# A hybrid decoder trunk on one core: the masks of the attention scores added in PSUM by VectorE in fp32, in place of matmuls of identity and mask

## The chip, the cores and the metric

The kernel runs on one core of a Trainium2 chip. The metric is the device time of one execution in microseconds; the runs of the kernel before took 1051.38, 1052.3 and 1052.58 us, a median of 1052.3. All inputs and the output are fp32.

## The reference

Two layers over 256 tokens of width 1024. Each layer has four sub-layers, each between two RMS norms: a SwiGLU feed-forward of width 2816, a mixer, a second feed-forward, and a gated embedding. The mixer is the part that the change touches:

```python
# eight MLA heads, causal; scores in fp32
s = (einsum('bqhd,bkhd->bhqk', qn, k_nope) + einsum('bqhd,bkd->bhqk', qr, k_rope)) * scale
s = where(causal, s, NEG)            # NEG = -1e30
w = softmax(s); o = einsum('bhqk,bkhd->bqhd', w, v)
# eight heads of dilated windows: (window, dilation) of (128, 1), (512, 4), (2048, 16)
for window, dilation in DIL_CONFIGS:
    ...
    s = where(valid, s, NEG); lse = m + log(den)
o = sum over configs of softmax(lse) * o_config
merged = concat(rmsnorm(o_mla), rmsnorm(o_dil)); return merged @ w_out
```

With 256 tokens each token of a dilated head sees the keys that any of the three configurations admits, weighted by how many of them do; the kernel computes it as one softmax whose exponentials are multiplied by that count.

## The kernel before

The tokens lie in two tiles of 128 (t = 0 and 1). Activations and weights are split into hi + lo parts of 12 significant bits (fp32r), and a product is three matmuls: hi by hi, lo by hi, hi by lo (`mm3`, lines 320 to 323; `proj`; lines 479 and on for the feed-forward's second product). The class `Weights` loads a raw tile by SyncE's queue, and a "tick" splits one piece of it: ScalarE writes hi (line 152), VectorE writes lo (line 153). Each phase of matmuls is emitted by `run`, and a table PLAN, written by hand, says after which step of the phase a tick falls, and after which step other work (transposes, copies) is put in. The order on every engine is the order of emission; each engine works through its queue in that order. `split_t` transposes 128x128 blocks through PSUM ("tp"), ScalarE copies them to hi (xh, line 401) and VectorE takes the difference (xl, line 402).

PSUM has two pools of four banks of 512 fp32 columns: ps_mm (tag "mm") and ps_acc. A matmul into a bank waits until the last reader of the tile that had it is done.

In the mixer, `scores(kind, t)` is called four times in a layer: "m" 0, "m" 1, "d" 0 and "d" 1, called m0, m1, d0 and d1 below. For t = 0 a bank holds 4 heads of 128 keys, for t = 1 two heads of 256 keys: 2, 4, 2 and 4 banks. For each bank TensorE first opens it with a matmul of a bf16 identity and the bf16 mask (lines 654 and 658): for "m" and for t = 0 the causal mask on the last 128 keys of each head, for d1 the mask on all 256 keys. It then adds the heads' scores to that (line 666). In the dilated calls two banks are worked on together, since their heads lie on the two halves of the 128 partitions. VectorE takes the maximum (mx, line 669) and scales it (line 670), and ScalarE the exponentials (p, line 673).

`p_t` transposes the probabilities (line 683); its copies out of PSUM (pt) are on ScalarE or VectorE for "m" (line 204 or 202), and for "d" a product with the counts on VectorE (lines 688 and 692). `p_v` multiplies with the values (o, line 706); VectorE takes the reciprocal of the sums (rc, line 711) and divides (om, line 716), ScalarE sums the squares (junk, line 354), GpSimd makes the norm's factor (rs, line 348), and VectorE scales (on, line 720). `o_t` transposes that into xh and xl. Around d1 the emission is: `p_v("d", 0)`; `scores("d", 1)`; the first half of the output product of tile 1 (f) with a tick after its step 5, `o_t("d", 0)` at step 6 and `p_t("d", 1)` at step 7; `p_v("d", 1)`.

Other names in the rows: kmt and qmt are the transposed keys and queries of the MLA heads, kdt and qdt those of the dilated heads, dt their transposes in PSUM, km and qm what is transposed, vm and vd the values, dk and dv the projections of the dilated keys and values, qu and ku the MLA up-projections.

`setup_late` loads the mask and the tables once, in the first feed-forward, and casts identity and mask to bf16 (lines 296 and 297).

## Time and profile before

| | |
|---|---|
| median of the runs | 1052.3 us |
| span of the profiled execution | 1052.4 us |
| instructions | 13069 |
| TensorE clock granted | 0.999 |
| DMA, mean | 180 GB/s |
| VectorE busy | 645.8 us, 61% |
| ScalarE busy | 528.9 us, 50% |

The span runs from the first to the last instruction. An engine's busy time is the time in which one of its instructions runs; matmuls overlap in the pipeline, so their listed durations add up to more than the time they take, and the distance of their starts is the better measure. The mean of a group is in nanoseconds, all else in microseconds. A row of the timeline has the start, the duration, the engine, the line of the kernel, the instruction with out<-in, the shape, the count of merged instructions, and in brackets the idle time of the engine just before, with what ended it. "issue" there is time for which the profile shows no wait. PE is TensorE, PEld its weight loads, DVE VectorE, ACT ScalarE, POOL GpSimd.

### The profile page before, as it was taken

How to read it: one execution, taken by the hardware profiler on the slowest of the kernel's cores; microseconds unless marked ns; L12 is line 12 of the kernel's file. 1: busy time of each engine (PE TensorE's matmuls, PEld its weight loads, DVE VectorE, ACT ScalarE, POOL GpSimd, SP SyncE). 2: the span in 40 equal slices, each digit the busy share in tenths (PEclk: the TensorE clock that was granted, in tenths of full speed). 3: DMA queues.
4: the chain of work that ended last, by engine and by line, in shares of the span. 5: the costliest groups of instructions: out<-in, count | busy, mean ns of one | idle time of the engine just before them, and what ended most of it. 6: DMA issues, size and time to landing. Idle time of an engine off the chain costs nothing.

```text
span 1052.4 us, 13069 instructions
## 1 busy us (share of the span) xinstructions
PE 1037.1 (99%) x5168; PEld 867.0 (82%) x5168; DVE 645.8 (61%) x819; ACT 528.9 (50%) x744; POOL 51.1 (5%) x123
## 2 busy tenths in 40 slices
PE   8999999999999999999999999999999999999997
PEld 5889888878888898888878888888888888988886
DVE  4765554778677455456776545557877864555474
ACT  5544443555556444444665444445564654444463
POOL 0000000210020000000110000002000200000011
PEclk9999999999999999999999999999999999999999
DMA  8864546364227564554547645455532575545601
GB/s 321 304 227 168 193 164 211 106 222 160 82 94 272 191 213 160 201 200 160 200 160 259 212 169 200 153 163 168 180 120 82 190 275 184 198 162 172 227 21 40
DMA packets 86158, 189.02 MB, mean 180 GB/s; under 512 B 3665, under 2 KB 15313, under 8 KB 86098
## 3 DMA queue, kind: packets, MB, share of 16 engines
q1 hardware_dynamic: 86098, 188.20, 52.0%
q8 instruction: 40, 0.66, 0.2%
q14 instruction: 20, 0.16, 0.0%
HBM read 187.13 MB, written 1.05 MB: 179 GB/s over the span
## 4 chain that ended last, share of the span: by engine, by line
PE 92%; DVE 3%; ACT 2%; DMA 1%; issue 1%; POOL 0%; SPq 0%; DVEq 0%; POOLq 0%; ACTq 0%
PE acc L479 23%; PE u L323 8%; PE u L321 8%; PE u L322 8%; PE g L321 7%; PE g L323 7%; PE g L322 7%; PE tp L398 3%; PE o L706 2%; PE sc L666 1%; DVE lo L153 1%; PE gt L323 1%; PE gt L322 1%; PE gt L321 1%; PE f L321 1%; PE f L323 1%
## 5 line engine op out<-in xcount | busy, mean ns | idle before, releaser
L153 DVE TENSOR_TENSOR lo<-raw,hi 128x1024 fp32r<-128x1024 f32 (+1 forms) x338 | 405.1, 1214 | 204.2 <-ACT hi L152 194.1
L152 ACT ACTIVATE hi<-raw 128x1024 fp32r<-128x1024 f32 (+1 forms) x338 | 347.2, 1049 | 170.9 <-PE u L323 79.3
L479 PE MATMUL acc<-hi,hid 128*128 128x512 f32 x704 | 201.5, 392 | 0.0
L479 PEld LDWEIGHTS acc<-hi,hid 128*128 128x128 f32 x704 | 131.7, 188 | 27.4
L321 PE MATMUL u<-hi,xh 128*128 128x512 f32 (+1 forms) x384 | 145.3, 379 | 0.0
L323 PE MATMUL u<-hi,xl 128*128 128x512 f32 (+1 forms) x384 | 143.2, 373 | 0.0
L322 PE MATMUL u<-lo,xh 128*128 128x512 f32 (+1 forms) x384 | 143.0, 372 | 0.0
L321 PE MATMUL g<-hi,xh 128*128 128x512 f32 (+1 forms) x360 | 135.0, 375 | 2.3 <-ACT xh L401 2.3
L323 PE MATMUL g<-hi,xl 128*128 128x512 f32 (+1 forms) x360 | 134.6, 374 | 0.0
L322 PE MATMUL g<-lo,xh 128*128 128x512 f32 (+1 forms) x360 | 134.5, 374 | 0.0
L479 PE MATMUL acc<-lo,hid 128*128 128x512 f32 x352 | 118.3, 395 | 0.0
L323 PEld LDWEIGHTS u<-hi,xl 128*128 128x128 f32 x384 | 72.3, 188 | 13.0
L322 PEld LDWEIGHTS u<-lo,xh 128*128 128x128 f32 x384 | 72.4, 188 | 12.1
L321 PEld LDWEIGHTS u<-hi,xh 128*128 128x128 f32 x384 | 72.3, 188 | 12.0
L321 PEld LDWEIGHTS g<-hi,xh 128*128 128x128 f32 x360 | 68.5, 190 | 14.4 <-ACT xh L401 2.7
L322 PEld LDWEIGHTS g<-lo,xh 128*128 128x128 f32 x360 | 68.5, 190 | 12.3 <-DVE lo L153 0.5
L323 PEld LDWEIGHTS g<-hi,xl 128*128 128x128 f32 x360 | 68.4, 190 | 12.4 <-DVE xl L402 0.6
L479 PEld LDWEIGHTS acc<-lo,hid 128*128 128x128 f32 x352 | 66.2, 188 | 13.2
L401 ACT ACTIVATE hid<-tp 128x512 fp32r<-128x512 f32 (+1 forms) x48 | 27.0, 563 | 95.6 <-PE tp L398 95.6
L453 DVE SCALAR_TENSOR_TENSOR hm<-u,rs,silu 128x512 f32<-128x512 f32 (+1 forms) x48 | 33.7, 703 | 65.1 <-PE u L323 65.1
L448 ACT ACTIVATE silu<-g,rs 128x512 f32<-128x512 f32 (+1 forms) x48 | 31.3, 652 | 81.3 <-PE g L323 81.2
L402 DVE TENSOR_TENSOR hid<-tp,hid 128x512 fp32r<-128x512 f32 (+1 forms) x48 | 31.0, 647 | 44.0 <-ACT hid L401 43.6
(216 smaller groups left out, 1195.0 us busy)
## 6 DMA issues: line engine op xcount, KB each, us to landing
raw<-in_ffn_up SPq DMA_DIRECT2D x44, 1024.0 KB, 5.1
raw<-in_ffn_down SPq DMA_DIRECT2D x44, 1024.0 KB, 5.0
raw<-in_ffn_gate SPq DMA_DIRECT2D x43, 1024.0 KB, 5.2
raw<-in_w_in SPq DMA_DIRECT2D x12, 1024.0 KB, 5.2
raw<-in_w_out SPq DMA_DIRECT2D x8, 1024.0 KB, 5.1
raw<-in_w_ple_gate SPq DMA_DIRECT2D x8, 1024.0 KB, 5.1
gain<-in_norm_gains SPq DMA_DIRECT2D x15, 512.0 KB, 4.0
raw<-in_w_in SPq DMA_DIRECT2D x4, 832.0 KB, 5.2
```

The source lines that it names most:

```text
L152: self.nc.scalar.activation(hv, raw, AF.Copy)
L153: self.nc.vector.tensor_tensor(lv, raw, hv.bitcast(F32), op=ALU.subtract)
L321: nc.tensor.matmul(ps, sh, wh, start=first, stop=False)
L322: nc.tensor.matmul(ps, sh, wl, start=False, stop=False)
L323: nc.tensor.matmul(ps, sl, wh, start=False, stop=last)
L398: nc.tensor.transpose(ps[:, j * P : (j + 1) * P], src[:, (b0 + j) * P : (b0 + j + 1) * P], ident)
L401: nc.scalar.activation(hv, v, AF.Copy)
L402: nc.vector.tensor_tensor(dl[:, k0 + b0 : k0 + b0 + nb, :], v, hv.bitcast(F32), op=ALU.subtract)
L448: nc.scalar.activation(s[:, :w], ps[:, :w], AF.Silu, scale=rx[t][:, 0:1])
L453: nc.vector.scalar_tensor_tensor(hm[:, :w], ps[:, :w], rx[t][:, 0:1], sg[t][:, c0 : c0 + w], op0=ALU.mult, op1=ALU.mult)
L479: nc.tensor.matmul(accs[t][n], hid[t][x][:, b, :], ws[w][:, 0, n * 512 : (n + 1) * 512], start=first and x + w == 0, stop=final and x == 1)
L706: nc.tensor.matmul(dst, pt[:, b * P : (b + 1) * P], va[:, kb, hd, :], start=kb == 0, stop=kb == t)
```

## The change

The bank's first matmul is no longer that of identity and mask. Each head's score matmul opens its own columns, and before the maximum VectorE adds the mask, now kept in fp32, to the bank in place. The bf16 identity and the casts go; the mask is loaded straight into its fp32 tile. All else in the diff is comments, so line numbers behind it are up to six lower in the changed kernel.

```diff
-    identb = const.tile([P, P], BF16, name="identb")
-    mask = const.tile([P, 2, P], BF16, name="mask")
+    mask = const.tile([P, 2, P], F32, name="mask")
...
-        mask32 = k2("mask32")[:, : 2 * P]
-        nc.sync.dma_start(mask32, a["mask"].rearrange("p c q -> p (c q)"))
+        nc.sync.dma_start(mask.rearrange("p c q -> p (c q)"), a["mask"].rearrange("p c q -> p (c q)"))
...
-        nc.vector.tensor_copy(identb, ident)
-        nc.vector.tensor_copy(mask.rearrange("p c q -> p (c q)"), mask32)
...
-                for v in vs:
-                    if kind == "m" or t == 0:
-                        nc.tensor.matmul(v[:, :, nk - P :], identb, mask[:, 1, None, :].to_broadcast([P, n, P]),
-                                         start=True, stop=True)
-                    else:
-                        mk = mask.rearrange("p c q -> p (c q)")[:, None, :].to_broadcast([P, n, nk])
-                        nc.tensor.matmul(v, identb, mk, start=True, stop=True)
...
-                        nc.tensor.matmul(v[:, i, :], q, k, start=False, stop=True, skip_group_check=True)
+                        nc.tensor.matmul(v[:, i, :], q, k, start=True, stop=True)
                 for v in vs:
                     mx = stat.tile([P, 4], F32, tag="mx", name="mx")
+                    if kind == "m" or t == 0:
+                        d, mk = v[:, :, nk - P :], mask[:, 1, None, :].to_broadcast([P, n, P])
+                    else:
+                        d, mk = v, mask.rearrange("p c q -> p (c q)")[:, None, :].to_broadcast([P, n, nk])
+                    nc.vector.tensor_tensor(d, d, mk, op=ALU.add)
                     nc.vector.tensor_reduce(mx[:, :n], v, axis=AX.X, op=ALU.max)
```

The order of VectorE at the end of d1 in layer 0, in the kernel before (mx from the last two banks, then the split of a weight, the low part of `o_t("d", 0)`, and the products of `p_t("d", 1)`):

```order
L669 TENSOR_REDUCE mx<-sc 128x2
L670 TENSOR_SCALAR mx<-mx 128x2
L669 TENSOR_REDUCE mx<-sc 128x2
L670 TENSOR_SCALAR mx<-mx 128x2
L153 TENSOR_TENSOR lo<-raw_2131,hi 128x1024
L402 TENSOR_TENSOR xl_112<-tp,xh_110 128x512
L692 TENSOR_TENSOR pt<-pt,mult 128x512 x4
```

The same place in the change:

```order
L662 TENSOR_TENSOR sc<-sc,mask 128x512
L663 TENSOR_REDUCE mx<-sc 128x2
L664 TENSOR_SCALAR mx<-mx 128x2
L662 TENSOR_TENSOR sc<-sc,mask 128x512
L663 TENSOR_REDUCE mx<-sc 128x2
L664 TENSOR_SCALAR mx<-mx 128x2
L153 TENSOR_TENSOR lo<-raw_2127,hi 128x1024
L398 TENSOR_TENSOR xl_111<-tp,xh_109 128x512
L686 TENSOR_TENSOR pt<-pt,mult 128x512 x4
```

Each bank has one instruction more, ahead of its maximum, and the split, xl and pt stand behind all four of them.

The order of TensorE through the second half of d1 in layer 0, before:

```order
L658 MATMUL sc<-mask,identb 128x512
L666 MATMUL sc<-kdt,qdt 128x256 x4
L658 LDWEIGHTS identb
L658 MATMUL sc<-mask,identb 128x512
L658 LDWEIGHTS identb
L658 MATMUL sc<-mask,identb 128x512
L666 MATMUL sc<-kdt,qdt 128x256 x4
L321 MATMUL f_2498<-hi,xh_111 128x512
```

And in the change, with the last products of `p_v("d", 0)` ahead:

```order
L319 MATMUL f_2369<-hi,xl_111 128x512
L700 MATMUL o_2431<-vd,pt 128x65 x4
L700 MATMUL o_2432<-vd,pt 128x65 x4
L655 MATMUL sc<-kdt,qdt 128x256 x8
L317 MATMUL f_2494<-hi,xh_110 128x512
```

The scores of all four banks follow one another without matmuls on other rows between them.

The order of VectorE around m0 in layer 0, before (from the rotary part of the queries to the copy of qmt):

```order
L534 TENSOR_TENSOR qm<-r_2009,r_2010 128x4x32
L669 TENSOR_REDUCE mx<-sc 128x4
L670 TENSOR_SCALAR mx<-mx 128x4
L669 TENSOR_REDUCE mx<-sc 128x4
L670 TENSOR_SCALAR mx<-mx 128x4
L202 COPY qdt<-dt 128x512
L202 COPY kmt<-kmt 96x4x128 x2
L202 COPY qmt<-qmt 96x512
```

In the change:

```order
L530 TENSOR_TENSOR qm<-r_2005,r_2006 128x4x32
L662 TENSOR_TENSOR sc<-sc,mask 128x512
L663 TENSOR_REDUCE mx<-sc 128x4
L664 TENSOR_SCALAR mx<-mx 128x4
L662 TENSOR_TENSOR sc<-sc,mask 128x512
L663 TENSOR_REDUCE mx<-sc 128x4
L664 TENSOR_SCALAR mx<-mx 128x4
L202 COPY qdt<-dt 128x512
L202 COPY kmt<-kmt 96x4x128 x2
L202 COPY qmt<-qmt 96x512
```

The copies of kmt and qmt stand behind two adds more.

## Prediction

> **What bounds the kernel now.** I read the page first, then the waits of TensorE, then the order of time around the scores in both layers.

> ```profile
> span 1052.4 us, 13069 instructions
> PE 1037.1 (99%) x5168; PEld 867.0 (82%) x5168; DVE 645.8 (61%) x819; ACT 528.9 (50%) x744; POOL 51.1 (5%) x123
> PE 92%; DVE 3%; ACT 2%; DMA 1%; issue 1%; POOL 0%; SPq 0%; DVEq 0%; POOLq 0%; ACTq 0%
> ```

> The span of the profiled execution is 1052.4 us, the median of the runs 1052.3, so I make the sum on the span and take it for the time as it is. TensorE is busy nearly always and holds 92% of the chain that ended last: whatever holds it up is paid in full, and a matmul less is a gain if no wait eats it. VectorE is busy for 61% on the average, but the average does not decide. TensorE's own waits do:

> ```profile
> PE pt L683 <- DVE xl L402: 0.8, 2, 0.4
> ```

> Twice in the run, once in each layer, TensorE stands at the transposes of the probabilities until VectorE is done. That is behind the second scores of the dilated heads (d1 below; m0, m1, d0, d1 are the four calls of scores in their order). Here is the place in layer 0, from the timeline (start, duration, engine, line, instruction, idle time before it):

> ```profile
> 286.92 0.75 DVE L720 SCALAR_TENSOR_TENSOR on<-om,rs,grp 128x512 f32<-128x512 f32 x1 [1.76 <-POOL rs L348]
> 287.58 0.68 DVE L669 TENSOR_REDUCE mx<-sc 128x2 f32<-128x512 f32 x1
> 288.30 0.17 DVE L670 TENSOR_SCALAR mx<-mx 128x2 f32<-128x2 f32 x1
> ...
> 288.57 3.23 ACT L673 ACTIVATE p<-sc,mx 128x256 f32<-128x256 f32 x8 [2.59 <-DVE mx L670]
> ...
> 290.69 0.17 DVE L670 TENSOR_SCALAR mx<-mx 128x2 f32<-128x2 f32 x1
> ...
> 291.68 1.06 ACT L152 ACTIVATE hi<-raw 128x1024 fp32r<-128x1024 f32 x1
> ...
> 292.77 1.22 DVE L153 TENSOR_TENSOR lo<-raw,hi 128x1024 fp32r<-128x1024 f32 x1 [1.91 <-ACT hi L152]
> 292.79 1.47 PE L683 MATMUL pt<-ident,p 128*128 128x128 f32 x12
> 293.92 0.68 DVE L402 TENSOR_TENSOR xl<-tp,xh 128x512 fp32r<-128x512 f32 x1
> 294.51 2.47 DVE L692 TENSOR_TENSOR pt<-pt,mult 128x512 f32<-128x512 f32 x4
> 294.65 0.66 PE L683 MATMUL pt<-ident,p 128*128 128x128 f32 x4 [0.40 <-DVE xl L402]
> ```

> The reader is to see one chain without a gap: four pairs of reduce and scale on VectorE, the exponentials of the last bank on ScalarE, the weight split hi behind them in ScalarE's queue, its lo on VectorE, xl behind that, and only then the last four transposes, because xl is what empties their PSUM bank. Anything put between the reduces moves 294.65 by as much. The second of the two waits is the same place in layer 1.

> **What TensorE gets back.** The 24 matmuls of identity and mask go, 12 in each layer. A matmul's price here is the distance of starts, since its listed duration overlaps the next:

> ```profile
> 240.88 0.38 PE L654 MATMUL sc<-mask,identb 128*128 128x512 bf16 x1
> 241.10 1.05 PE L666 MATMUL sc<-kmt,qmt 96*128 96x128 f32 x8
> ...
> 258.72 0.27 PE L654 MATMUL sc<-mask,identb 128*128 128x256 bf16 x1
> 258.83 1.03 PE L666 MATMUL sc<-kmt,qmt 96*128 96x256 f32 x4
> ```

> ```profile
> 270.33 0.59 PE L654 MATMUL sc<-mask,identb 128*128 128x512 bf16 x2
> 270.86 1.16 PE L666 MATMUL sc<-kdt,qdt 64*128 64x128 f32 x16
> ...
> 284.22 0.59 PE L658 MATMUL sc<-mask,identb 128*128 128x512 bf16 x2
> 284.74 1.13 PE L666 MATMUL sc<-kdt,qdt 64*128 64x256 f32 x8
> 285.81 0.60 PE L658 MATMUL sc<-mask,identb 128*128 128x512 bf16 x2
> 286.35 1.13 PE L666 MATMUL sc<-kdt,qdt 64*128 64x256 f32 x8
> ```

> m0 has two at 0.22 (0.44), m1 four at 0.11 (0.44), d0 a pair in 0.53, d1 two pairs in 0.52 and 0.54 (1.06): 2.47 us in a layer, 4.9 in all. The pairs cost more than 2 x 0.22: between matmuls on all rows and those on 64 rows the weight loads have a gap, here before the second pair:

> ```profile
> 285.81 0.11 PEld L658 LDWEIGHTS <-identb 128*128 128x128 bf16 x2 [0.33 <-issue]
> ```

> [...] The row has a gap at this place, and nothing in the sum of the forecast hangs on it.

> **What VectorE takes on.** Sixteen adds of 512 columns and eight of 256 (m1) in PSUM, with the mask broadcast from SBUF. No row of this kernel shows VectorE writing PSUM. The nearest have one operand in PSUM and write SBUF:

> ```profile
> L153 DVE TENSOR_TENSOR lo<-raw,hi 128x1024 fp32r<-128x1024 f32 x326 | 393.5, 1222 | 199.1 <-ACT hi L152 189.2
> L716 DVE TENSOR_TENSOR om<-o,rc 128x256 f32<-128x256 f32 x16 | 6.8, 424 | 0.6
> L692 DVE TENSOR_TENSOR pt<-pt,mult 128x512 f32<-128x512 f32 x8 | 4.9, 679 | 0.0
> ```

> So 0.68 us for 512 columns and 0.42 for 256. The reduce must wait for the add's result, as the scale waits for the reduce, and that pair starts 0.72 apart (287.58 to 288.30) for a duration of 0.68. I take 0.72 and, by the same 0.04, 0.46. From below: 0.61, the distance of starts of the four L692 (2.47 / 4), if the wait costs nothing. From above: 1.22, the row with twice the elements, if reading and writing one bank went in turns. I take 0.72 because L692 is the same operation on the same tile shape but for where it writes. The 24 adds make 14.9 us of VectorE.

> By the order shown with the change, all four adds of d1 stand on VectorE between on and lo, each ahead of its bank's reduce; lo, xl and the products pt are queued behind them, and TensorE waits for xl. So d1 costs 4 x 0.72 = 2.88 us in each layer. TensorE's 1.06 us saved in d1 buy nothing: at 286.92 the chain starts from on, not from the scores.

> Whether the 1.41 us saved before that (m0, m1, d0) bring the chain forward is the second term. I follow them through.

> m0, two adds, 1.44 us:

> ```profile
> 243.41 0.68 DVE L669 TENSOR_REDUCE mx<-sc 128x4 f32<-128x512 f32 x1
> ...
> 245.67 2.17 ACT L673 ACTIVATE p<-sc,mx 128x128 f32<-128x128 f32 x8
> 245.76 1.28 DVE L202 COPY kmt<-kmt 96x512 f32<-96x512 f32 x2
> ...
> 247.22 1.03 PE L607 MATMUL qmt<-ident,qm 128*96 128x128 f32 x8
> ...
> 249.93 2.36 DVE L153 TENSOR_TENSOR lo<-raw,hi 128x1024 fp32r<-128x1024 f32 x2 [1.39 <-ACT hi L152]
> ```

> The reduce starts when VectorE comes free, not when the scores end. The kmt copies move to 247.2, the first done at 247.84. The second four of the qmt transposes, due at 247.65 - 0.44 = 247.2, need the bank of that copy: TensorE loses 0.65 and stands at +0.2 against before. The exponentials start one add later, 0.7, and as lo already waits for ScalarE, VectorE goes on 0.7 late.

> m1, four adds of 0.46, 1.84 us:

> ```profile
> 265.04 0.17 DVE L670 TENSOR_SCALAR mx<-mx 128x2 f32<-128x2 f32 x1
> ...
> 266.03 0.60 ACT L401 ACTIVATE xh<-tp 128x512 fp32r<-128x512 f32 x1
> ...
> 266.66 0.69 DVE L402 TENSOR_TENSOR xl<-tp,xh 128x512 fp32r<-128x512 f32 x1 [1.45 <-ACT xh L401]
> ...
> 268.59 1.91 PE L683 MATMUL pt<-ident,p 128*128 128x128 f32 x16
> 268.79 0.69 ACT L616 ACTIVATE vd<-dv,rs 128x512 f32<-128x512 f32 x1 [1.21 <-PE dv L323]
> ```

> The last scale, xh and xl come 0.7 + 1.84 = 2.5 later; xl ends near 269.9. vd had 1.21 to spare and comes 1.3 later, done near 270.75. TensorE arrives at the transposes at +0.2 - 0.44 = -0.24. Its third four (due 269.46 - 0.24) wait for xl's bank until 269.9, its fourth for vd's until 270.75, against 269.9 before: +0.85. The scores of d0 lose their masks (0.53) but wait for ScalarE's copies of pt behind vd, also 1.3 later, which eats that again. So TensorE enters the next products at about +0.9. There VectorE waits for TensorE:

> ```profile
> 275.77 0.18 DVE L711 RECIPROCAL rc<-o 128x4 f32<-128x4 f32 x1 [1.14 <-PE o L706]
> ```

> This wait of 1.14 and the room before it take in d0's two adds, and the chain to 286.92 runs on at +0.9. In all 0.9 + 2.88 = 3.8 us in a layer, 7.6 in two: 1052.4 + 7.6 = **1060.0 us**. The two casts that leave the set-up ran under TensorE's first feed-forward matmuls, and the wait for DMA there falls to the copy of the positions: nothing.

> **The rivals.** *The early waits don't come* (my assignment of banks in m0 and m1 is wrong, and their delays fall in slack). Then the chain enters d1 1.41 early: 2.88 - 1.41 = 1.5 in a layer, 1055.3 us; with adds at 0.61 it is 1.0, 1054.5. For it: TensorE shows no wait at all at these places before. Against: the slack I find there is at most vd's 1.21 us, and the adds bring 1.4 to 2.5.

> *A dear write to PSUM.* At 1.26 an add in chain, d1 costs 5.0, and the early part grows by an add in m0 (0.54) and four halves in m1 (1.1): 7.5 in a layer, 1067.4 us; half-way it is 1063.7. For it: nothing shown. Against: reads from PSUM cost no more than reads from SBUF here.

> *Not slower: the last transposes wait for their data alone.* If the bank behind 294.65 was free before xl, they need only the exponentials, which end at 291.8. With the adds that is 291.8 + 2.88 - 1.41 = 293.3 if the early waits stay away as well, 1.35 ahead of before: 1049.7 us; with the early waits it is 1054.3, and between lies no change. It decides at 2.85 us, the distance from the last exponential to the transposes: below that, d1's adds are free. Against: 294.65 falls on the end of xl within 0.1. *Everything is hidden* would give 1052.4 - 4.9 = 1047.5, and needs VectorE to have room at d1, where the rows have none. [...]

> **How the numbers follow.** Forecast 0.55, early waits absent 0.20, dear PSUM write 0.12, data alone 0.08 (mostly no change), all hidden 0.05. The likeliest gives 1060.0. The range runs from 1054.5, the lower rival's end, to 1064.0, a little over half-way to the dearest add; outside lie the two rivals below and a third of the dear one, 0.17. A measurement here tells about 0.2%, 2.1 us, from no change. Faster by more 0.06, within 0.08, slower 0.86.

> **What would show it.** In the changed profile: a group of sc from sc and mask near 0.68 and 0.42 us; the distance from on to the last scale in d1 up by 2.9; the wait of the last pt transposes on xl up from 0.4 to some 3 us in each layer; short new waits at qmt and at pt of m1. Wrong would be an add far from 0.7, a last pt that starts before xl ends, or the time between on of d1 and the products of m0 shrunk by the masks. Wrong in sign is a total below 1050.

## The result, and the profile after

The changed kernel takes 1069.59 us (median of 5 runs, 1065.09 to 1071.97), the kernel before 1052.3 beside it (5 runs, 1051.21 to 1056.54): the ratio is 1.0149, with a 95% interval of 1.0132 to 1.0165. It is slower, as forecast, but by 17 us where 8 were forecast, and it lies outside the range. One run of the experiment e5 below took 3701.98 us and is left out of its ratio. The page of the profiled execution, whose own time is 1067.54 us:

```profile
span 1065.8 us, 13048 instructions
PE 1042.6 (98%) x5144; PEld 872.4 (82%) x5144; DVE 659.0 (62%) x841; ACT 528.9 (50%) x744; POOL 50.6 (5%) x123
PEclk9999999999989999999999999999998999999999
PE 85%; DVE 8%; ACT 3%; DMA 2%; issue 1%; POOL 1%; SPq 0%; DVEq 0%; POOLq 0%; ACTq 0%
```

TensorE's share of the chain that ended last falls from 92% to 85%, VectorE's grows from 3% to 8%. And the row of the granted clock has two slices with an 8. Before, it had none:

```profile
PEclk9999999999999999999999999999999999999999
```

Although 24 matmuls are gone, TensorE is busy for 5.5 us more (1042.6 against 1037.1). Both facts say the same: some matmuls ran slowly. Now its waits:

```profile
PE pt L677 <- DVE xl L398: 4.2, 4, 2.0
PE pt L677 <- ACT p L667: 3.5, 4, 0.9
...
PE qmt L603 <- DVE kmt L202: 0.9, 2, 0.4
```

The wait of the pt transposes on xl has grown from 0.8 in all to 4.2, new waits of pt on the exponentials p make 3.5, and qmt waits for the bank of kmt, 0.9. The adds themselves, from the groups:

```profile
L662 DVE TENSOR_TENSOR sc<-sc,mask 128x512 f32<-128x512 f32 x16 | 11.1, 694 | 0.4 <-PE sc L655 0.4
L662 DVE TENSOR_TENSOR sc<-sc,mask 128x256 f32<-128x256 f32 x8 | 3.4, 427 | 0.0
```

0.69 and 0.43 us: writing PSUM in place costs about what writing SBUF did in the kernel before (0.68 and 0.42). Here is d1 of layer 0, the place that the prediction showed, from the timeline:

```profile
286.71 0.75 DVE L714 SCALAR_TENSOR_TENSOR on<-om,rs,grp 128x512 f32<-128x512 f32 x1 [1.76 <-POOL rs L344]
287.38 0.69 DVE L662 TENSOR_TENSOR sc<-sc,mask 128x512 f32<-128x512 f32 x1
288.11 0.69 DVE L663 TENSOR_REDUCE mx<-sc 128x2 f32<-128x512 f32 x1
...
293.05 0.66 PE L677 MATMUL pt<-ident,p 128*128 128x128 f32 x4 [0.87 <-ACT p L667]
...
294.58 1.12 PE L677 MATMUL pt<-ident,p 128*128 128x128 f32 x4 [0.87 <-ACT p L667]
295.50 1.23 DVE L153 TENSOR_TENSOR lo<-raw,hi 128x1024 fp32r<-128x1024 f32 x1 [1.91 <-ACT hi L152]
296.64 0.68 DVE L398 TENSOR_TENSOR xl<-tp,xh 128x512 fp32r<-128x512 f32 x1
297.38 1.12 PE L677 MATMUL pt<-ident,p 128*128 128x128 f32 x4 [1.69 <-DVE xl L398]
...
299.58 4.50 PE L700 MATMUL o<-vd,pt 128*128 128x65 f32 x32
303.89 0.48 PE L317 MATMUL f<-hi,xh 128*128 128x512 f32 x1
```

From on to the last transposes it is 297.38 - 286.71 = 10.67 us; before it was 294.65 - 286.92 = 7.73. The chain is 2.94 longer, for a forecast of 2.88. But look at the durations of TensorE: four transposes take 0.66 at 293.05 and 1.12 at 294.58. The products o took 3.68 before:

```profile
295.85 3.68 PE L706 MATMUL o<-vd,pt 128*128 128x65 f32 x32
...
299.33 0.48 PE L321 MATMUL f<-hi,xh 128*128 128x512 f32 x1
```

From the last transposes to the first f behind o it was 299.33 - 294.65 = 4.68, and is 303.89 - 297.38 = 6.51: 1.83 us more behind the end of the wait, with the same instructions. The windows name the cause (columns: stretch, length, busy us and count of PE, PEld, DVE, ACT, POOL, then the granted clock, the DMA share and GB/s):

```profile
292.00:294.00 2.00, 0.83 (x6) 0.42 (x4) 1.52 (x4) 1.15 (x3) 0.00 (x0) 1.00 0.00 0
294.00:296.00 2.00, 1.12 (x4) 0.72 (x4) 0.50 (x1) 2.00 (x5) 0.00 (x0) 0.61 0.00 0
296.00:298.00 2.00, 0.62 (x3) 0.62 (x4) 2.00 (x4) 0.90 (x1) 0.00 (x0) 0.50 0.00 0
298.00:300.00 2.00, 2.00 (x9) 1.71 (x7) 2.00 (x4) 0.00 (x0) 0.00 (x0) 0.50 0.00 0
300.00:302.00 2.00, 2.00 (x14) 2.00 (x14) 0.85 (x1) 0.00 (x0) 0.00 (x0) 0.68 0.16 14
...
814.00:817.00 3.00, 1.34 (x8) 0.84 (x8) 1.26 (x3) 2.31 (x5) 0.00 (x0) 0.95 0.00 0
817.00:820.00 3.00, 0.99 (x6) 0.88 (x5) 2.76 (x4) 1.64 (x3) 0.00 (x0) 0.50 0.00 0
820.00:823.00 3.00, 3.00 (x14) 2.71 (x12) 2.59 (x4) 0.00 (x0) 0.00 (x0) 0.50 0.00 0
823.00:826.00 3.00, 3.00 (x16) 3.00 (x15) 0.00 (x0) 0.00 (x0) 0.00 (x0) 0.50 0.61 229
826.00:829.00 3.00, 3.00 (x14) 2.81 (x13) 1.21 (x4) 0.00 (x0) 0.00 (x0) 0.50 0.32 126
829.00:832.00 3.00, 3.00 (x12) 2.43 (x11) 1.32 (x2) 1.67 (x3) 0.74 (x2) 0.77 0.01 3
```

The granted clock of TensorE falls from 1.00 to 0.50 while it waits for the exponentials and xl, and stays there after the wait. A mean of 0.61 over 2 us puts the fall near 294.4 in layer 0, 0.68 the return near 301.3: 6.8 us. In layer 1 it is 816.7 to 830.4: 13.7 us. While TensorE waits the half clock costs nothing, afterwards half of what it still lasts: from 297.38 to 301.3 that is 3.9 / 2 = 2.0 us in layer 0, from 819.12 to 830.4 it is 11.3 / 2 = 5.6 in layer 1. These two are estimates; the table below has what was measured, 1.88 and 5.27. In layer 1 the products o run at half speed to their end (3.68 before):

```profile
819.12 1.12 PE L677 MATMUL pt<-ident,p 128*128 128x128 f32 x4 [2.01 <-DVE xl L398]
...
821.32 6.92 PE L700 MATMUL o<-vd,pt 128*128 128x65 f32 x32
```

So the whole difference can be laid out by following the same instruction through both traces (change less before, in us, at both layers; the start of a layer's mixer is its first product za):

| from, to | layer 0 | layer 1 |
|---|---|---|
| up to the start of the mixer (layer 1: from o_t(d, 1) of layer 0) | -0.77 | -0.08 |
| mixer, up to on of d1: masks less early waits | +0.56 | +0.57 |
| on of d1 to its last pt transposes: four adds | +2.94 | +2.93 |
| from there on, at half clock | +1.88 | +5.27 |

The -0.08 is what lies between the two mixers. All of it makes 13.3 us, and the spans differ by 13.4; the 0.1 left over lies behind the second mixer. The half clock is 7.15 of that, more than half. The other four runs have a mean clock of 0.986 to 0.989, the profiled one 0.989; those at 0.986 are the slowest (1069.6 to 1072.0).

### The profile page after: what moved, and what is told of

The parts are those of the page before. It is cut to its first block, busy times and chain, and to the rows that moved or that the text cites. A ratio compares the mean times of both kernels' runs of the same rounds, so it can differ in the third digit from the quotient of the medians.

```text
span 1065.8 us, 13048 instructions
## 1 busy us (share of the span) xinstructions
PE 1042.6 (98%) x5144; PEld 872.4 (82%) x5144; DVE 659.0 (62%) x841; ACT 528.9 (50%) x744; POOL 50.6 (5%) x123
## 3 DMA queue, kind: packets, MB, share of 16 engines
HBM read 187.13 MB, written 1.05 MB: 177 GB/s over the span
## 4 chain that ended last, share of the span: by engine, by line
PE 85%; DVE 8%; ACT 3%; DMA 2%; issue 1%; POOL 1%; SPq 0%; DVEq 0%; POOLq 0%; ACTq 0%
PE acc L475 23%; PE u L319 8%; PE u L317 8%; PE u L318 8%; PE g L317 7%; PE g L318 7%; PE g L319 7%; PE tp L394 3%; DVE lo L153 2%; PE o L700 2%; DVE mx L663 1%; DMA latg<-in_kv_norm 1%; DVE sc L662 1%; PE f L317 1%; PE f L318 1%
## 5 line engine op out<-in xcount | busy, mean ns | idle before, releaser
L153 DVE TENSOR_TENSOR lo<-raw,hi 128x1024 fp32r<-128x1024 f32 (+1 forms) x338 | 405.1, 1214 | 203.0 <-ACT hi L152 192.8
L152 ACT ACTIVATE hi<-raw 128x1024 fp32r<-128x1024 f32 (+1 forms) x338 | 347.2, 1050 | 169.0 <-PE u L319 79.3
```

The source lines that it names most:

```text
L152: self.nc.scalar.activation(hv, raw, AF.Copy)
L153: self.nc.vector.tensor_tensor(lv, raw, hv.bitcast(F32), op=ALU.subtract)
```

## The experiments

The letters of the theories are those of the expectations. In all of them theory A holds that what counts is the chain to the last transposes of d1 (and, in e1 to e5, that the clock falls when TensorE stands still there, which is the cost beyond the adds). Its rivals put the loss down to something else: VectorE's total work, the write into PSUM, the matmuls that are gone, or a clock that falls for other reasons. The first four kernels ran on one chip (before there: 1053.02), the last four on another (before: 1052.72).

**e1: the changed kernel, with TensorE kept busy in d1.** Products with a matrix of zeros, added to a bank in use, fill the waits of the pt transposes:

```diff
+    zr = const.tile([P, P], F32R, name="zr")
...
+        nc.vector.tensor_scalar(zr, ident, 0.0, None, op0=ALU.mult)
...
         def p_t(kind, t):
             for g in range(len(groups(kind, t))):
                 p = S["p", kind, t][g]
+                if kind == "d" and t == 1:
+                    for _ in range((0, 4, 4, 9)[g]):
+                        nc.tensor.matmul(S["f", 1][1], zr, xl[1][:, :4, :], start=False, stop=False)
                 ps = bank("pt")
```

> The changed kernel with 17 more matmuls in each layer, of a zero matrix into the open sum f, put between the four groups of transposes of d1 (4, 4 and 9), where TensorE waits. They add zeros, so the output is the same. Theory A (VectorE's longer chain, then TensorE's clock falls to half because TensorE stood idle): the chain to the last transposes stays 2.7 to 3.5 us late in each layer, the granted clock stays at 1.00 there, and the time is 1052.3 + 6.2 = 1058.5 us (1057 to 1060.5). Theory B (the chain sets all, the clock's fall is chance or comes from something else): the time stays near 1068, and the clock still shows 0.5 behind d1.

Measured: 1060.02 us, ratio 1.0066 (1.0049 to 1.0083), mean clock 0.997 to 0.999. The timeline of layer 0:

```profile
292.63 0.66 PE L682 MATMUL pt<-ident,p 128*128 128x128 f32 x4
293.04 2.35 PE L679 MATMUL f<-xl,zr 128*128 128x512 f32 x9
295.44 0.66 PE L682 MATMUL pt<-ident,p 128*128 128x128 f32 x4
...
296.63 3.68 PE L705 MATMUL o<-vd,pt 128*128 128x65 f32 x32
```

Transposes and products are back at 0.66 and 3.68. The adds still cost +2.95 and +2.93 from on to the last pt, and behind it nothing is lost (-0.01 and +0.01). More work on TensorE saves 9.6 us against the change, though the kernel before is 0.7 slower on this chip: the clock is the cause of what the change loses beyond its waits, and the waits are what brings the clock down. The time came out 1.5 above what A expected, inside its range. The kernel before being 0.7 slower on this chip is a part of that. In the profiled run, the slowest of the four, the start of layer 1's mixer cost more: za waits 2.55 us for r there (0.81 before), and the clock stands at 0.50 from 733.58 to 736.99.

**e2: the changed kernel, with d1's masks back on TensorE.** m0, m1 and d0 keep their adds (the tiles' declarations and the start flags of the scores are left out here):

```diff
+                by_pe = kind == "d" and t == 1
+                if by_pe:
+                    for v in vs:
+                        mk = maskb.rearrange("p c q -> p (c q)")[:, None, :].to_broadcast([P, n, nk])
+                        nc.tensor.matmul(v, identb, mk, start=True, stop=True)
...
                     if kind == "m" or t == 0:
                         d, mk = v[:, :, nk - P :], mask[:, 1, None, :].to_broadcast([P, n, P])
-                    else:
-                        d, mk = v, mask.rearrange("p c q -> p (c q)")[:, None, :].to_broadcast([P, n, nk])
-                    nc.vector.tensor_tensor(d, d, mk, op=ALU.add)
+                        nc.vector.tensor_tensor(d, d, mk, op=ALU.add)
```

> The changed kernel, but the four banks of d1 get their mask by the matmuls of identity and mask as before; m0, m1 and d0 keep the adds. Theory A: only the adds of d1 cost; the other 16 fall into slack, so the time is 1052.6 us (1051 to 1054) and the clock stays at 1.00. Theory C (the prediction's second term: the adds of m0 and m1 make waits that d1 inherits): 0.9 us more in each layer, 1054.1. Theory B' (each add costs its share): two thirds of the loss, 1062.

Measured: 1055.68 us, ratio 1.0019 (1.0007 to 1.0032), mean clock 0.996 to 0.999. From the start of the mixer to on of d1 the trace of layer 0 loses 0.58, and from on to the last pt the layers lose 0.01 and 0.00. So nearly all of the loss is d1's, and the 16 early adds, which theory A had put into slack, cost some 0.6 in a layer: nearer to the 0.9 of theory C. In layer 1 the stretch up to on loses 2.11. The clock accounts for the difference of 1.5: it stands at 0.50 from 730.60 to 734.02, behind a wait of 1.73 us of za for r, and half of these 3.4 us is 1.7. Why za waits longer there than in the kernel before (0.81) isn't shown.

**e3: the changed kernel, with the weight split moved.** One entry of the plan, (5, 7) to (7, 8), lets the split hi and lo come after xl, so that xl is next on VectorE behind the last scale:

```diff
-    "wo10": ((5, 7), (6, 7)), ...
+    "wo10": ((7, 8), (6, 7)), ...
```

> The changed kernel with one split of a weight moved from step 5 to step 8 of the phase behind d1, so that its hi (0.95 us on ScalarE) and lo (1.22 us on VectorE) no longer stand between the exponentials and xl. Theory A: the last transposes start some 2.2 us earlier, 0.5 to 1.3 us late against the kernel before; if that keeps the clock up the time is 1054 us (1053 to 1055.5), if the two shorter waits before still bring the clock down it is 1057 to 1061. Theory B (VectorE's total time): the same work is done, so 1068.

Measured: 1057.35 us, ratio 1.0041 (1.0026 to 1.0056), mean clock 0.996. Its waits:

```profile
PE pt L677 <- ACT p L667: 3.5, 4, 0.9
PE pt L677 <- DVE xl L398: 1.7, 4, 0.6
```

From on to the last pt it is +1.35 and +1.34 in place of 2.94. The waits on the exponentials are those of the change, that on xl is 0.6 in place of 1.7 and 2.0. The clock fell in layer 0 (0.66 over 295 to 300, 1.57 us lost behind the last pt) and not in layer 1 (0.01), though the waits are the same in both: 0.87, 0.87 or 0.88, and 0.56. The time is the second of A's two cases. The waits alone don't say when the clock falls; the next section comes back to these two layers.

**e4: the kernel before, with four spare products on VectorE in d1.** All masks stay matmuls; one product of the scores' size goes from PSUM to a spare bf16 tile in SBUF ahead of each reduce, and nothing reads it:

```diff
                     mx = stat.tile([P, 4], F32, tag="mx", name="mx")
+                    if kind == "d" and t == 1 and len(pts) < 4:
+                        nc.vector.tensor_tensor(spare.rearrange("p (n k) -> p n k", n=n), v,
+                                                mult.rearrange("p c q -> p (c q)")[:, None, :].to_broadcast([P, n, nk]), op=ALU.mult)
                     nc.vector.tensor_reduce(mx[:, :n], v, axis=AX.X, op=ALU.max)
```

> The kernel before, all masks by matmul, with four products more on VectorE in d1, one ahead of each maximum, that read the bank and write a spare tile in SBUF. Nothing waits for them. Theory A: the chain in d1 is four times 0.61 to 0.72 us longer and TensorE waits that much: 1052.3 + 2 x 2.6 = 1057.5 us if the clock holds, 1062 to 1067 if the wait brings it down as in the change. Theory D (the write into PSUM or the lacking matmuls are what costs): no more than 1054.

Measured: 1062.87 us, ratio 1.009 (1.0066 to 1.0115). Of its ten runs two took 1057.12 and 1057.18 at a mean clock of 0.998, seven 1061.7 to 1064.9 at 0.992 to 0.994, and one, the profiled one, 1071.2 at 0.986. One program, and its time goes by its clock. Timeline and windows of layer 0:

```profile
292.68 0.66 PE L687 MATMUL pt<-ident,p 128*128 128x128 f32 x4 [0.41 <-ACT p L677]
295.49 1.12 PE L687 MATMUL pt<-ident,p 128*128 128x128 f32 x4 [2.15 <-DVE xl L403]
```

```profile
295.00:300.00 5.00, 4.51 (x19) 4.22 (x19) 3.96 (x6) 0.01 (x1) 0.00 (x0) 0.50 0.01 1
300.00:305.00 5.00, 5.00 (x24) 4.90 (x24) 0.93 (x4) 0.00 (x0) 0.00 (x0) 0.50 0.55 212
```

The chain is 2.39 longer in each layer, and behind it 6.13 and 4.82 us go at half clock. No mask is added in PSUM here and no matmul left out, so the fall needs neither. VectorE's delay in front of xl is enough.

**e5: the same with two products.** `len(pts) < 2` in place of `< 4`.

> The kernel before with two (not four) products more on VectorE in d1 of each layer, that write a spare tile. Theory A: the last transposes start 2 x 0.6 = 1.2 us later in each layer, so 1054.7 us if the clock holds. A wait of some 1.9 us in one piece then stands ahead of the last transposes, and if that brings the clock down in a layer it costs 2 to 6 us more there, and the single times lie apart by that. Theory B (the clock's fall has nothing to do with the length of the wait): falls as often as with four, 1060 to 1063.

Measured: 1055.42 us, ratio 1.0024 (1.0012 to 1.0035), mean clock 0.997 to 0.999. The chain grows by 1.20 and 1.19, as A expected for a clock that holds. The wait is longer than in the kernel before, and the clock holds:

```profile
PE pt L687 <- DVE xl L403: 3.2, 2, 1.6
```

So the loss per product isn't even: two cost 2.7 us, four 9.9, since the clock joins in between.

**e6: the kernel before, without any mask on the dilated heads.** The counts that the probabilities are multiplied with are zero there:

```diff
-                    if kind == "m" or t == 0:
+                    if kind == "m":
                         nc.tensor.matmul(v[:, :, nk - P :], identb, mask[:, 1, None, :].to_broadcast([P, n, P]),
                                          start=True, stop=True)
-                    else:
-                        mk = mask.rearrange("p c q -> p (c q)")[:, None, :].to_broadcast([P, n, nk])
-                        nc.tensor.matmul(v, identb, mk, start=True, stop=True)
...
-                        nc.tensor.matmul(v[:, i, :], q, k, start=False, stop=True, skip_group_check=True)
+                        nc.tensor.matmul(v[:, i, :], q, k, start=kind == "d", stop=True, skip_group_check=kind == "m")
```

> The kernel before without any mask on the dilated heads' scores: neither matmul nor add. The product with the counts of keys, which is zero where a key is not seen, masks the exponentials already; the maximum is then taken over all keys of the block. No add on VectorE at all. Theory A: TensorE saves 0.53 us in d0, which brings the chain forward by as much, and 1.06 us in d1, which only makes its wait ahead of the last transposes longer (0.75 to 1.8 us): 1052.3 - 2 x 0.53 = 1051.2 us if the clock holds, 1054 to 1062 if the longer wait brings it down. Theory B (only VectorE's adds make the loss): 1049 to 1051.2, clock 1.00.

Measured: 1051.47 us, ratio 0.9988 (0.998 to 0.9997), mean clock 0.996 to 0.999.

```profile
PE pt L680 <- DVE xl L402: 3.2, 2, 1.6
```

TensorE reaches the transposes earlier and waits there for xl: of the matmuls saved in d1 nothing is left, as the prediction said of the change. What is gained is 0.43 and 0.44 us ahead of on. The time is near theory A's 1051.2, but theory B's range ends there too, so it is this wait that speaks for A. The clock holds through a wait of 1.6 us here too.

**e7: e6 and the edit of e3 together.**

> As e6_no_d_mask, and the split of a weight moved from step 5 to step 8 behind d1, out of the chain to the last transposes. Theory A: that chain ends at the exponentials, one copy and one difference, 292.4 us where before had 294.65, and TensorE itself arrives at 292.3, so the whole saving of TensorE counts, with its old wait: 0.53 + 1.06 + 0.75 = 2.3 us in a layer, 1047.7 us (1046.5 to 1049), and the clock stays at 1.00. Theory B (VectorE's total work sets the time): 1051 to 1052.

Measured: 1047.09 us, ratio 0.9953 (0.9936 to 0.997): the fastest of all, 5.6 us under the kernel before on its chip. No wait at pt is left in its trace, and theory A's 1047.7 came out. Work taken off TensorE and work taken off VectorE's chain pay only together.

**e8: the kernel before with the edit of e3 alone.**

> The kernel before with the split of that weight moved from step 5 to step 8, and nothing else. Theory A: the wait of 0.75 us ahead of the last transposes goes in each layer, 1050.8 us (1050 to 1051.8). Theory B: no change, 1052.3.

Measured: 1052.43 us, ratio 0.9994 (0.998 to 1.0007): no difference shown, so the 1.5 us that theory A expected don't appear in the time. The waits at pt are gone and, counted from on, o comes 0.62 us earlier in layer 0 and 0.63 in layer 1. But in the profiled run, at 1054.41 one of the slower ones, the start of layer 1's mixer ate it, with a wait of za for r (2.35 us where the kernel before has 0.81) and a clock of 0.50 from 731.22 to 734.62:

```profile
PE za L321 <- DVE r L533: 3.2, 2, 2.4
```

## Why the prediction was right in direction and wrong in size

**The adds' price** was right: 0.69 and 0.43 measured, 0.72 and 0.46 taken with the distance to the reduce (287.38 to 288.11 is 0.73). By the prices taken the 24 adds make 15.2 us and not the 14.9 that the prediction names; nothing hangs on it.

**The chain of d1** was right: 2.88 forecast, 2.94 and 2.93 measured, and 2.95 and 2.93 in e1 with the clock at full. TensorE's matmuls saved there bought nothing, as said. The wait on xl came out at 1.7 to 2.0 us in place of "some 3": the rest of it stands earlier, in the waits of pt on the exponentials, which the prediction didn't list.

**The early waits** were right in kind and 0.3 us too large: 0.9 forecast, 0.56 measured, 0.58 in layer 0 of e2. The waits at qmt are in the trace (0.4 each), and those of m1's pt on xl, at 0.26 and 0.27. The 0.85 that the prediction worked out there was too much: the last group of these transposes, which was to wait for vd, shows no wait. The rival by which they don't come, 1055.3, falls with them.

**The step that failed** is this one: "whatever holds it up is paid in full". The sum took a wait as costing its own length, and then let TensorE go on as before. It goes on at half speed: 1.88 us in layer 0, 5.27 in layer 1, and the prediction has no term for that. The clock's row of before is all 9, and no wait there at pt was over 0.4, so no row gave the price. What could be seen beforehand is that the forecast put 3 us of waiting into a stretch in which TensorE had never waited for more than 0.4: a state that the trace of before doesn't show, and whose cost had to be bounded. All matmuls up to a return of the clock at half speed would have been such a bound, and the range had none. e1, the change without the fall in d1, measures 1060.02, which the sum of 7.0 (2 x 3.50, the two middle rows of the table) and the kernel before on that chip make too: 1053.02 + 7.0. That it is also the number forecast is luck in part: the early term was 0.7 too large over both layers, the kernel before is 0.6 slower on that chip than the 1052.4 that the forecast starts from, and the profiled run holds a fall of the clock at the start of layer 1's mixer, which nobody forecast.

**The rival with the dear write to PSUM** gave 1067.4, close to the measured time, and is wrong: it needs 1.26 us for an add. A total that fits doesn't prove a mechanism. "The last transposes wait for their data alone" and "everything is hidden" fall with the wait on xl, which stands as forecast.

**When the clock falls** can't be told from the waits:

| kernel | waits at pt of d1 in a layer, us | TensorE busy in the emptiest stretch of 3.41 us of d1, layer 0 and 1, us | clock |
|---|---|---|---|
| before | 0.4 | 3.01, 3.01 | held |
| e5 | 1.6 | 2.53, 2.02 | held |
| e6 | 1.6 | 1.79, 1.79 | held |
| e3 | 0.87, 0.87, 0.56 | 1.31, 2.15 | fell in layer 0 only |
| e4, profiled run | 0.41, 2.15 | 1.48, 1.26 | fell in both; two of ten runs show 0.998 over the span |
| the change | 0.87, 0.87, 1.7 to 2.0 | 1.78, 1.67 | fell in both; all five runs at 0.986 to 0.989 |

It isn't the length of one wait: in e3 it fell with none over 0.9, and in e5 a single wait of 2.67 us left it at 1.00 (the timeline, and the windows of the ten us around it):

```profile
731.79 0.42 PE L322 MATMUL za<-hi,xh 128*128 128x416 f32 x1 [2.67 <-DVE r L534]
```

```profile
730.00:740.00 10.00, 8.09 (x42) 7.19 (x43) 7.85 (x16) 4.23 (x9) 1.76 (x3) 1.00 0.56 161
```

The traces do hold a part of the answer, in the times at which the clock changes. Windows of 0.05 us place each change: in the change it falls at 294.46 and 816.70 and returns at 301.28 and 830.36. Six of the ten traces have more than one change, 24 in all, and within each trace their distances are whole multiples of 3.413 us, to within 0.03 us. From fall to fall here it is 153 of them (522.24 us), and the half clock lasts two in layer 0 (6.82 us) and four in layer 1 (13.66 us); in d1 of e4 it lasts four and three, in e3 one. So the third column of the table goes by stretches of 3.413 us in line with the changes, and not by single waits: it has the time, of 3.41 us, in which TensorE was busy in the emptiest such stretch of d1 at full clock. Where a stretch lies is an estimate, carried on in steps of 3.413 us from the changes in the same trace (before, e5, e6 and e7 have only one, at the end of the run). In e3 the same three waits fall into one stretch in layer 0 and into two in layer 1:

```profile
291.60:295.01 3.41, 1.31 (x8) 0.83 (x8) 1.89 (x5) 2.72 (x6) 0.00 (x0) 1.00 0.00 0
295.01:298.42 3.41, 3.34 (x13) 3.06 (x14) 3.41 (x6) 1.18 (x2) 0.00 (x0) 0.50 0.00 0
810.42:813.83 3.41, 2.15 (x13) 1.21 (x11) 2.77 (x6) 2.03 (x6) 0.00 (x0) 1.00 0.00 0
813.83:817.25 3.42, 2.38 (x17) 2.01 (x17) 2.47 (x5) 2.81 (x5) 0.00 (x0) 1.00 0.00 0
```

The wait of za for r agrees: stretches with 0.74 (e1), 1.61 (e8) and 1.64 (e2) busy end in a fall, and e5's wait of 2.67 is cut into two with 2.05 and 2.00.

**What stays open** is the exact condition. In d1 the clock fell with 1.78 and held with 1.79, but elsewhere stretches with 1.57 (before, from 1043.83) and 1.73 (e7, from 210.44) passed without a fall, so the busy time can't be all that counts. Leaving the transposes out of it doesn't help: in e6 the stretch from 806.14 holds next to nothing else, and the clock held. Nor is a full stretch enough for the return: in layer 1 of the change those from 820.11 and from 823.52 are busy throughout (3.41 and 3.42) and the clock stays at 0.50. They hold mostly the products o, which have only 65 columns; it returns with the next stretch, in which o ends and the products f go on. That o counts for less would fit, but no run tests it.

## What to carry to other kernels

Where the bounding engine is TensorE, price a new wait twice: its length, and the matmuls behind it at half clock (here 1.88 and 5.27 us), as long as no experiment rules that out. The longest wait doesn't tell: waits of 0.87, 0.87 and 0.56 us ended in a fall in layer 0 of e3, and one of 2.67 in e5 didn't. Here the work in stretches of 3.413 us told more, though not all (a fall with 1.78 us busy, none with 1.57). And read the granted clock over the few us around, not the mean of the span: the change has 0.50 from 294.46 to 301.28 and 0.989 over the span. Matmuls that are saved ahead of a wait come back only when the chain that is waited for is shortened as well (e6 alone 0.9988, with the split moved 0.9953). And if work must go to the engine that TensorE waits for, look first for one that can be left out altogether.

## What the runs showed of the hardware

With 17 products with a matrix of zeros in each layer (e1) the clock was 1.00 in d1: from 292 to 301 in layer 0, from 815 to 824 in layer 1.
